# Leaving the first softmax map unscaled: a change to a hybrid SSD and differential-attention layer on one core

## The chip, the cores and the metric

The kernel runs on one core of a Trainium2 chip. A core has a matrix engine (TensorE, "PE" in the profile, its weight loads "PEld"), three engines for elementwise work (VectorE "DVE", ScalarE "ACT", GpSimd "POOL") and SyncE ("SP"), which here issues the DMA transfers. The metric is the device time of one execution in microseconds (us); lower is better.

## The reference, cut to what matters

The layer normalises its input, projects it, feeds an SSD (state space) half and an attention half, and multiplies the two halves, side by side, with an output matrix; a residual and a last LayerNorm follow. The change is in the attention half. Of it:

```python
def diff_attention(q, k, v, lam, slopes):
    ...
        probs = jax.nn.softmax(scores, axis=-1)
        w = probs[:, :, 0] - lam * probs[:, :, 1]
        return jnp.einsum("bhqs,bshe->bqhe", w.astype(v.dtype), v)
...
def rms_norm(x, g):
    xf = x.astype(jnp.float32)
    ms = jnp.mean(jnp.square(xf), axis=-1, keepdims=True)
    return (xf * lax.rsqrt(ms + RMS_EPS) * g).astype(x.dtype)
...
    o = diff_attention(q, k, v, lam, slopes)
    o = rms_norm(o, subln_g) * (1.0 - lam_init)
    y_attn = o.reshape(b, s, D_ATTN) * jax.nn.silu(g)
    mix = jnp.einsum("bse,ed->bsd", jnp.concatenate([y_ssm, y_attn], axis=-1), w_out.astype(h.dtype))
    return layer_norm(ALPHA * h + mix, ln_g, ln_b)
```

There are 8 attention heads, 1024 tokens, and 128 value channels for each head. Since the norm divides a head's output by its own root mean square, a factor that is the same for all channels of a token falls out of it, but for the epsilon that is added under the root.

## The kernel before

The program is written as lanes of work (generators), and a helper, the Loom, weaves them into one order of TensorE's instructions. Each lane emits instructions and yields the tiles that it needs next; the Loom keeps books of when each tile would be ready by its own cost estimates, and lets go on the first lane, by a table of ranks (`LANES`), whose next piece would not make TensorE wait. TensorE's order is pinned to that result; the other engines' order is set by the tile scheduler. All instructions go through one wrapper, so nearly all rows of the profile carry its line, L140, and are told apart by their tiles.

From 432 us on the program is attention, then the output projection. For each head and each block of 128 queries (`tb`, 8 per head, 64 in all) the lanes are:

- `scores` (L977): 8 matmuls into the two PSUM tiles `sc`; on VectorE a custom operation for each map (`p<-sc,dist`: ALiBi distance and row extremum `nm`); on ScalarE an Exp for each map (`p<-p,nm`), which leaves the row sums in `ls`.
- `combine` (L1012): `rs` is the reciprocal of the two sums, its second column times minus lambda; the first map `p0` is scaled by its reciprocal (on GpSimd; on ScalarE in head 7); then one VectorE instruction adds the second map (`p0 = p1*rs1 + p0`).
- `values` (L1028): 8 transposes of `p0` through a PSUM bank `bk`, a rounded copy `wh` on ScalarE and the rest `wl` on VectorE; after two blocks 24 matmuls (8 times `vh` with `wh`, `vh` with `wl`, `vl` with `wh`) give the head's output `o` for 256 queries.
- `finish` (L1066): after four blocks the RMS norm: the square `osq`, split into `osh` and `osl`, two matmuls with a matrix of ones (`ones_r`), the mean plus epsilon in `msq`, Ln and Exp for the root, one Newton step, gate and store (`yd<-o`).

Between these the Loom places what other work there is: until the end of head 6 the input projection of later heads (`bk<-hh,whi` and the like, weights loaded as `wst` and split by GpSimd into `wlo`), and after that the output projection `project_out` (L1241) in units of 128 tokens times half of the rows (`bk<-oh,oyh`; `ws` are its weight rows, split into `oh`/`ol` and `or`; `ys` its inputs, split into `oyh`/`oyl`). A unit of the first five token blocks sums in two PSUM banks, which are then added into the residual tile `xr` on VectorE, and this frees the banks. `xr` is the input, normalised on ScalarE, times `g_e`, plus `b_e` (two rows broadcast by DMA, then scaled once on ScalarE), both on GpSimd. The tiles `g_e`, `b_e` stand where tiles of the attention stood before, so their loads wait for those to be read.

```python
A.activation(p0, p0, AF.Copy, scale=rs[:, 0:1])                       # head 7
P.tensor_scalar(p0, p0, rs[:, 0:1], 1.0, op0=ALU.mult, op1=ALU.mult)  # other heads
yield p0
V.scalar_tensor_tensor(p0, p1, rs[:, 1:2], p0, op0=ALU.mult, op1=ALU.add)
```

Of the kernel before, what the change touches and what calls it, by code (L numbers as in the profile page):

```python
# [9 lines left out]
F32 = mybir.dt.float32  # L10
# [4 lines left out]
ALU = mybir.AluOpType  # L15
# [12 lines left out]
# rank of each lane, and how much later than estimated it takes its inputs to be ready  # L28
# [18 lines left out]
class Loom:  # L47
    """Weaves lanes of work into one instruction order.

    A lane is a generator that emits instructions and yields in between: nothing (it can go on),  # L50
    a tile (it can go on once the tile's last write is done), a function (once it holds) or a
    time (it lets other lanes go first for so long).
    When each tile is ready is estimated from the instructions emitted so far; the lane that
    goes on is the first one, by rank, that would not make TensorE wait."""
# [30 lines left out]
    def slot(self, key, start, cost):  # L85
        """The first gap of an engine that takes an instruction ready at start."""
        busy = self.busy.setdefault(key, [])
        i = len(busy)
        while i and busy[i - 1][1] > start:
            i -= 1  # L90
        while i < len(busy) and busy[i][0] - start < cost:
            start = max(start, busy[i][1])
            i += 1
        busy.insert(i, (start, start + cost))
        del busy[:-300]
        return start
# [33 lines left out]
class Engine:  # L130
    """An engine whose instructions are noted in the loom."""
# [21 lines left out]
class Pool:  # L153
    """A tile pool whose slots' reuse is noted in the loom; under are the pools whose place it takes."""
# [62 lines left out]
def hybrid_layer_kernel(  # L217
# [48 lines left out]
    # -|query - key| for every offset of a block of 128 queries  # L266
    dist = const.tile([128, 1920], F16, name="dist")

# [27 lines left out]
    class Block:  # L296
        """128 projected channels; evac(half, psum) takes each half of the sequence."""
# [8 lines left out]
    def weights():  # L306
        """Loads and splits the weights of a block while the one before it is computed."""
# [60 lines left out]
    # ================= embedding LayerNorm and bidirectional SSD =================  # L368
# [30 lines left out]
    def conv_block(b, when, dst_of, after):  # L399
        """Block b of x/B/C: raw projection, then convolution and SiLU into dst_of()."""  # L400
# [31 lines left out]
    def to_tokens(src, put):  # L432
        """Transposes src [128 ch, S]; put(half, psum [128 tokens, 4, 128])."""
# [48 lines left out]
    with tc.tile_pool(name="dp", bufs=1) as dp_, tc.tile_pool(name="p0", bufs=1) as p0_:  # L482
# [93 lines left out]
        def steps_lane():  # L576
            """Step sizes, decays and their sums within chunks."""
# [117 lines left out]
    def ssd(g):  # L695
# [72 lines left out]
        def maps():  # L768
            """Within-chunk maps of one head, four chunks at a time."""
# [96 lines left out]
    # ================= differential attention =================  # L866
# [8 lines left out]
    class Head:  # L875
        def __init__(self, h):
            self.pool = lambda: ep if h % 2 == 0 else att["op"]
            self.q, self.k, self.v, self.g = [], 0, 0, 0
            self.scored = self.summed = self.done = 0
# [3 lines left out]
    def free_since(h, what, n):  # L883
        """The tiles that head h overwrites are read no more."""
# [92 lines left out]
    def scores():  # L977
        """Unnormalised maps of 128 queries at a time."""
        for h, H in enumerate(heads_):
            m_h = 2.0 ** -(h + 1)  # L980
            for tb in range(8):
# [3 lines left out]
                ls = ap.tile([128, 2], F32, name="ls", bufs=2)  # L985
# [13 lines left out]
                for m in range(2):  # L999
# [6 lines left out]
                                 accum_out=ls[:, m:m + 1])  # L1006
# [5 lines left out]
    def combine():  # L1012
        """Difference of the two normalised maps, left in the first."""
        for _ in range(64):
# [3 lines left out]
            rs = ap.tile([128, 2], F32, name="rs", bufs=2)  # L1018
            V.reciprocal(rs, ls)
            V.tensor_mul(rs[:, 1:2], rs[:, 1:2], neg_lam)  # L1020
            if H is heads_[7]:
                A.activation(p0, p0, AF.Copy, scale=rs[:, 0:1])
            else:
                P.tensor_scalar(p0, p0, rs[:, 0:1], 1.0, op0=ALU.mult, op1=ALU.mult)
            yield p0
            V.scalar_tensor_tensor(p0, p1, rs[:, 1:2], p0, op0=ALU.mult, op1=ALU.add)
            maps_.append((H, tb, p0))

    def values():
        """Maps transposed and split; weighted sums of the values, 256 queries at a time."""  # L1030
        for _ in range(64):
# [31 lines left out]
            if n:  # L1063
                loom.add(finish(H, H.o, tb // 4))

    def finish(H, o, half):  # L1066
        """RMS norm over the head's 128 channels, gate, store."""
# [13 lines left out]
        V.tensor_scalar(ms, pms, 1.0 / 128, EPS, op0=ALU.mult, op1=ALU.add)  # L1081
# [4 lines left out]
        V.tensor_mul(ms, ms, rt)  # L1086
        V.tensor_scalar(ms, ms, -0.5, 1.5, op0=ALU.mult, op1=ALU.add)
        yield lambda: H.g == 1
        P.tensor_mul(o, o, H.gate[:, 512 * half:512 * half + 512])
        V.tensor_mul(rt, rt, ms)  # L1090
# [12 lines left out]
    # ================= output projection and LayerNorm =================  # L1103
# [3 lines left out]
    def late_rows():  # L1107
        """Places for the rows of the attention half: tiles of the last head, as they fall free."""
# [15 lines left out]
    def early_rows():  # L1124
        """The rows for the SSD half take the place of the normalised input."""
# [7 lines left out]
    def rows_out():  # L1133
        """Splits the rows of the output projection, half a row at a time."""
# [28 lines left out]
    def y_out():  # L1163
        """Splits the gated outputs of one unit, two units ahead of the products."""
# [20 lines left out]
    def residuals():  # L1185
        """ALPHA times the normalised input, token blocks in the order of their use."""
# [127 lines left out]
```

## Time and profile before

| | |
|---|---|
| time, 3 runs | 1234.62, 1236.5 and 1240.69 us; median 1236.5 |
| profiled execution | span 1236.1 us, which stands for its own time; 0.4 us below the median |
| busy, PE | 1176.0 us, 95% of the span |
| busy, DVE | 933.8 us, 76% |
| busy, ACT | 677.8 us, 55% |
| busy, POOL | 479.9 us, 39% |
| mean granted TensorE clock | 0.990 of full speed |
| chain that ended last | PE 11%, DVE 1%, all else under 1% of the span |

A busy share is the time in which an engine runs instructions; a wait is the idle time of an engine before an instruction, with the instruction that ended it. The clock is the share of full speed that TensorE was granted; where it reads near 0.5, matmuls take twice as long and still count as busy. The trace names an operation by its output and inputs, `p<-p,rs` for instance, with buffer numbers left out.

### The profile page before, as it was taken

Reading aid. Unit: us, or ns where it says so; the run is one execution under the profiler, and the core shown is the slowest. Engines: PE = TensorE matmul, PEld = TensorE weight load, DVE = VectorE, ACT = ScalarE, POOL = GpSimd, SP = SyncE. Lnnn points to the kernel's source line nnn. Section 1 sums busy time; section 2 is a strip of 40 time slices with the busy share of each in tenths; the row PEclk is TensorE's granted clock in tenths of the full one; section 3 lists DMA queues with packets and bytes.
Section 4 is the critical chain, followed back from the end, with each engine's and each line's share of the span. In section 5 each row is a group of like instructions: output and inputs, shape, how many; then the busy total and the mean of one; then the engine's idle time right before and its main releaser. Section 6 shows DMA issues by size and latency. Waiting matters only on the chain. (4 is left out here: it accounts for less than half of the span.)

```text
span 1236.1 us, 16398 instructions
## 1 busy us (share of the span) xinstructions
PE 1176.0 (95%) x5881; PEld 922.4 (75%) x5881; DVE 933.8 (76%) x1334; ACT 677.8 (55%) x1181; POOL 479.9 (39%) x404
## 2 busy tenths in 40 slices
PE   5998999899899999999999999999999998999997
PEld 3787666788567777777787777877777776778885
DVE  6687888867988568788788787887878889962334
ACT  4556356734457456665755656556656687641221
POOL 7422664323654323223332333233332429541354
PEclk9999999999899999999999999999999998999999
DMA  6113335522245421012112111121111263233221
GB/s 198 32 33 112 89 112 167 178 69 65 89 118 151 132 72 49 26 44 51 26 35 52 43 44 35 34 52 35 43 28 47 81 209 107 55 123 112 78 85 60
DMA packets 107591, 98.03 MB, mean 79 GB/s; under 512 B 9364, under 2 KB 79349, under 8 KB 107509
## 3 DMA queue, kind: packets, MB, share of 16 engines
q1 hardware_dynamic: 107509, 96.98, 27.2%
q8 instruction: 46, 0.75, 0.2%
q14 instruction: 36, 0.29, 0.1%
HBM read 75.85 MB, written 16.91 MB: 75 GB/s over the span
## 5 line engine op out<-in xcount | busy, mean ns | idle before, releaser
L140 PE MATMUL bk<-hh,whi 128*128 128x512 f32 x832 | 353.2, 425 | 0.6
L140 PE MATMUL bk<-hl,whi 128*128 128x512 f32 x832 | 327.0, 393 | 3.2 <-POOL hl L140 2.8
L140 PE MATMUL bk<-hh,wlo 128*128 128x512 f32 x832 | 328.0, 394 | 0.0
L140 ACT ACTIVATE p<-p,nm 128x1024 f32<-128x1024 f32 x128 | 146.8, 1148 | 121.7 <-DVE nm L140 121.0
L140 POOL TENSOR_TENSOR wlo<-wst,whi 128x512 fp32r<-128x512 f32 x104 | 161.5, 1557 | 126.9 <-ACT whi L140 109.2
L140 POOL TENSOR_SCALAR p<-p,rs 128x1024 f32<-128x1024 f32 x56 | 64.5, 1152 | 350.4 <-DVE rs L140 287.5
L140 PEld LDWEIGHTS bk<-hh,wlo 128*128 128x128 f32 x832 | 156.6, 188 | 34.9
L140 PEld LDWEIGHTS bk<-hl,whi 128*128 128x128 f32 x832 | 157.7, 190 | 32.9 <-POOL hl L140 5.4
L140 PEld LDWEIGHTS bk<-hh,whi 128*128 128x128 f32 x832 | 157.7, 190 | 32.7 <-issue 5.8
L140 DVE CUSTOM_DVE_ANT_0 p<-sc,dist 128x1024 f32<-128x1024 f32 x128 | 151.3, 1218 | 11.6 <-PE sc L140 10.9
L140 DVE SCALAR_TENSOR_TENSOR p<-p,rs,p 128x1024 f32<-128x1024 f32 x64 | 128.4, 2007 | 22.1 <-POOL p L140 18.0
L140 DVE TENSOR_TENSOR wl<-bk,wh 128x512 fp32r<-128x512 f32 x128 | 87.0, 684 | 15.6 <-ACT wh L140 13.7
L140 ACT CAST wh<-bk 128x512 fp32r<-128x512 f32 x128 | 74.1, 580 | 43.2 <-PE bk L140 42.7
L140 ACT CAST whi<-wst 128x512 fp32r<-128x512 f32 x104 | 64.2, 620 | 46.9 <-PE bk L140 38.1
L140 PE MATMUL bk<-ident,p 128*128 128x128 f32 x512 | 79.4, 278 | 4.7 <-DVE wl L140 2.7
L140 PEld LDWEIGHTS bk<-ident,p 128*128 128x128 f32 x512 | 61.6, 142 | 29.5 <-DVE wl L140 6.2
L140 PE MATMUL bk<-wh,vh 128*128 128x256 f32 x256 | 74.6, 291 | 0.0
L140 PE MATMUL bk<-wl,vh 128*128 128x256 f32 x256 | 72.2, 282 | 0.7 <-DVE wl L140 0.7
L140 PE MATMUL sc<-kk,q 128*128 128x512 f32 x256 | 72.3, 393 | 0.0
L140 PE MATMUL bk<-wh,vl 128*128 128x256 f32 x256 | 72.0, 281 | 0.0
L140 ACT ACT_TABLE_LOAD x42 | 53.9, 1283 | 25.5 <-DVE t L140 15.7
L140 PEld LDWEIGHTS bk<-xt,t 128*128 128x128 f32 x256 | 45.8, 192 | 26.5 <-issue 15.0
(217 smaller groups left out, 2188.1 us busy)
## 6 DMA issues: line engine op xcount, KB each, us to landing
wst<-in_w_in_dram SPq DMA_DIRECT2D x104, 256.0 KB, 3.0
t<-acs_d SPq DMA_DIRECT2D x64, 256.0 KB, 3.5
ws<-in_w_out_dram SPq DMA_DIRECT2D x32, 256.0 KB, 3.1
ys<-yd SPq DMA_DIRECT2D x32, 256.0 KB, 3.0
xb<-in_x_dram SPq DMA_DIRECT2D x8, 512.0 KB, 6.2
zd<-zs SPq DMA_DIRECT2D x16, 256.0 KB, 2.5
gz<-zd SPq DMA_DIRECT2D x16, 256.0 KB, 3.3
yd<-ys SPq DMA_DIRECT2D x16, 256.0 KB, 2.8
```

Of the source, the lines that this page charges most:

```text
L140: r = f(*args, **kw)
```

## The change

The first map stays as the exponentials are. With sums l0 and l1 the head's output is then l0 times what it was, if the second map is added with the factor -lambda * l0 / l1. The norm takes the factor l0 out again, when epsilon is multiplied by l0 squared. Since in `finish` channels lie on partitions and queries along the row, and in `scores` queries lie on partitions, the 512 values eps * l0^2 of four blocks go to DRAM (`ed`, one word each, turned) and come back as a row that is broadcast to all partitions (`er`).

In `scores` one tile `ls` of 4 x 2 sums now serves four blocks. In `combine` the scaling of `p0` and the yield behind it are gone; in `finish` `er` is added in place of the constant, and the Newton step is written in three instructions for four. The compiler object gets a smaller scratch for dynamic DMA. (Comments and docstrings also go; they are left out here.)

```diff
     def scores():
...
-                ls = ap.tile([128, 2], F32, name="ls", bufs=2)
+                if tb % 4 == 0:
+                    ls = ap.tile([128, 4, 2], F32, name="ls", bufs=2)
...
-                                 accum_out=ls[:, m:m + 1])
+                                 accum_out=ls[:, tb % 4, m:m + 1])
...
     def combine():
...
-            rs = ap.tile([128, 2], F32, name="rs", bufs=2)
-            V.reciprocal(rs, ls)
-            V.tensor_mul(rs[:, 1:2], rs[:, 1:2], neg_lam)
-            if H is heads_[7]:
-                A.activation(p0, p0, AF.Copy, scale=rs[:, 0:1])
-            else:
-                P.tensor_scalar(p0, p0, rs[:, 0:1], 1.0, op0=ALU.mult, op1=ALU.mult)
-            yield p0
-            V.scalar_tensor_tensor(p0, p1, rs[:, 1:2], p0, op0=ALU.mult, op1=ALU.add)
+            rs = ap.tile([128, 1], F32, name="rs", bufs=2)
+            V.reciprocal(rs, ls[:, tb % 4, 1:2])
+            V.scalar_tensor_tensor(rs, rs, ls[:, tb % 4, 0:1], neg_lam, op0=ALU.mult, op1=ALU.mult)
+            V.scalar_tensor_tensor(p0, p1, rs, p0, op0=ALU.mult, op1=ALU.add)
             maps_.append((H, tb, p0))
+            if tb % 4 == 3:
...
+                e2 = ap.tile([128, 4], F32, name="e2", bufs=2)
+                V.scalar_tensor_tensor(e2, ls[:, :, 0], EPS, ls[:, :, 0], op0=ALU.mult, op1=ALU.mult)
+                ed = dr.tile([4, 128], F32, name="ed", bufs=2)
+                with nc.allow_non_contiguous_dma(reason="512 words"):
+                    dma(ed.rearrange("t p -> p t"), e2)
+                er = ap.tile([128, 512], F32, name="er", bufs=2)
+                dma(er, ed.rearrange("t p -> (t p)").partition_broadcast(128))
+                H.er.append(er)
...
-                loom.add(finish(H, H.o, tb // 4))
...
+                loom.add(finish(H, H.o, H.er[tb // 4], tb // 4))
...
-        V.tensor_scalar(ms, pms, 1.0 / 128, EPS, op0=ALU.mult, op1=ALU.add)
+        V.scalar_tensor_tensor(ms, pms, 1.0 / 128, er, op0=ALU.mult, op1=ALU.add)
...
         V.tensor_mul(ms, ms, rt)
-        V.tensor_mul(ms, ms, rt)
-        V.tensor_scalar(ms, ms, -0.5, 1.5, op0=ALU.mult, op1=ALU.add)
+        V.scalar_tensor_tensor(ms, ms, -0.5, rt, op0=ALU.mult, op1=ALU.mult)
+        V.scalar_tensor_tensor(rt, ms, 1.5, rt, op0=ALU.add, op1=ALU.mult)
...
-        V.tensor_mul(rt, rt, ms)
...
-    nc = _bacc.Bacc("TRN2", target_bir_lowering=False, num_devices=1)
+    nc = _bacc.Bacc("TRN2", target_bir_lowering=False, num_devices=1,
+                     dynamic_dma_scratch_size=1024)
```

The Loom's books change with it, and so does the order. Two places follow, and one on SyncE.

**VectorE, the same block of the steady part (the 28th, the last of a half head).** Before, the custom operations of one block (`ISA` rows), then the reciprocal of the two sums and the addition of the maps, with a `wl` between them:

```order
L140 ISA p1_6204,nm_6189<-sc_6194,dist_80 128x1024
L140 ISA nm_6189 128x1
L140 RECIPROCAL rs_6260<-ls_6190 128x2
L140 TENSOR_TENSOR rs_6260<-rs_6260,neg_lam_83 128x1
L140 TENSOR_TENSOR wl_6239<-bk_6240,wh_6238 128x4x128
L140 SCALAR_TENSOR_TENSOR p0_6201<-p1_6204,rs_6260,p0_6201 128x1024
```

After, with the epsilon values `e2` ahead:

```order
L140 ISA p1_6271,nm_6257<-sc_6261,dist_80 128x1024
L140 ISA nm_6257 128x1
L140 SCALAR_TENSOR_TENSOR e2_6346<-ls_5985 128x4
L140 RECIPROCAL rs_6342<-ls_5985 128x1
L140 SCALAR_TENSOR_TENSOR rs_6342<-rs_6342,ls_5985,neg_lam_83 128x1
L140 SCALAR_TENSOR_TENSOR p0_6268<-p1_6271,rs_6342,p0_6268 128x1024
```

The reciprocal is of one column, the product takes l0 in as well, and nothing of another engine stands between `rs` and the addition.

**TensorE, end of head 6.** Before, the last of the 24 matmuls of head 6's values (`bk_8978`), then the last 24 projection matmuls (`bk_8984<-hh1_0...` to `hh1_7...`) with 8 transposes among them, then the ones matmuls (`osh`, `osl`), the scores, 4 transposes, and the first matmuls of an output unit (`bk_9246`, `bk_9247`):

```order
L140 MATMUL bk_8978<-wh_8886,vl_8046 128x256
L140 MATMUL bk_8984<-hh1_0_108,whi_8722 128x512
L140 MATMUL bk_8984<-hl1_0_124,whi_8722 128x512
...
L140 MATMUL bk_8984<-hl1_7_131,whi_8726 128x512
L140 MATMUL bk_8984<-hh1_7_115,wlo_8727 128x512
L140 MATMUL bk_9040<-osh_9036,ones_r_76 128x512
L140 MATMUL bk_9040<-osl_9037,ones_r_76 128x512
L140 MATMUL sc_9098<-kk_8598,q_8406 128x512 x2
L140 MATMUL sc_9101<-kk_8598,q_8406 128x512 x2
...
L140 MATMUL sc_9101<-kl_8599,q_8406 128x512
L140 MATMUL bk_9114<-ident_69,p0_8992 128x128 x4
L140 MATMUL bk_9246<-oh0_9126,oyh_9224 128x512
L140 MATMUL bk_9247<-oh1_9132,oyh_9224 128x512
```

After, the last of head 6's values is `bk_9160`; the output unit in these rows is the second one (`bk_9334`, `bk_9335`; the first, `bk_9028` and `bk_9029`, stands ahead of the values now):

```order
L140 MATMUL bk_9160<-wh_9055,vl_7892 128x256
L140 MATMUL bk_9217<-ident_69,p0_9123 128x128 x4
L140 MATMUL bk_9240<-ident_69,p0_9123 128x128 x4
L140 MATMUL bk_9214<-osh_9210,ones_r_76 128x512
L140 MATMUL bk_9214<-osl_9211,ones_r_76 128x512
L140 MATMUL sc_9255<-kk_8467,q_8267 128x512 x2
L140 MATMUL sc_9258<-kk_8467,q_8267 128x512 x2
...
L140 MATMUL sc_9258<-kl_8468,q_8267 128x512
L140 MATMUL bk_9271<-ident_69,p0_9173 128x128 x4
L140 MATMUL bk_9278<-ident_69,p0_9173 128x128 x4
L140 MATMUL bk_9334<-oh0_8908,oyh_9018 128x512
L140 MATMUL bk_9335<-oh1_8914,oyh_9018 128x512
```

The projections have been used up before this place, the first output unit has moved ahead of it, and the ones matmuls stand behind 8 transposes alone.

**SyncE, the same stretch, after.** Its issues in order; `ed_9069` and `er_9071` are head 6's last epsilon row, and the `ws` rows behind them are output weights (`ws_8978` and `ws_8984` of rows 14 and 15, which the first output unit's last matmuls use):

```order
L140 DMA ys_9218<-yd2_134 128x512
L140 DMA ys_9224<-yd2_134 128x512
L140 DMA ed_9069<-e2_9067 128x4x1
L140 DMA er_9071<-ed_9069 128x512
L140 DMA ws_8978<-in_w_out_dram 128x512
L140 DMA ws_8984<-in_w_out_dram 128x512
L140 DMA ws_8990<-in_w_out_dram 128x512
L140 DMA ys_9463<-yd3_135 128x512
L140 DMA ws_8996<-in_w_out_dram 128x512
L140 DMA ws_9002<-in_w_out_dram 128x512
L140 DMA ys_9469<-yd3_135 128x512
L140 DMA g_e_9302<-in_ln_emb_g_dram 128x1024
```

`ed` waits for `e2`, and `er` for `ed`'s landing; before, no such pair stood among the issues.

## Rows read from the trace of the kernel before

**Rows 1.** Busy time by stretch: core start:end, length, then us busy of each engine.
```profile
432.40:980.00 547.60, 545.59 (x2921) 430.28 (x2919) 439.14 (x658) 333.74 (x580) 166.96 (x123) 1.00 0.17 43
980.00:1000.00 20.00, 17.61 (x104) 13.97 (x104) 17.78 (x25) 13.63 (x24) 5.34 (x5) 1.00 0.43 133
1000.00:1031.50 31.50, 27.46 (x146) 21.91 (x146) 27.06 (x41) 28.91 (x47) 15.86 (x11) 0.99 0.71 234
1031.50:1038.00 6.50, 6.50 (x18) 5.25 (x19) 6.46 (x7) 4.89 (x8) 6.50 (x5) 0.54 0.25 82
...
1080.00:1087.45 7.45, 4.93 (x27) 3.77 (x25) 4.99 (x8) 4.99 (x8) 3.71 (x3) 1.00 0.65 208
1087.45:1092.50 5.05, 5.05 (x19) 4.17 (x20) 4.01 (x7) 2.31 (x4) 1.73 (x2) 0.66 0.40 124
1092.50:1228.30 135.80, 135.77 (x598) 110.41 (x596) 48.82 (x84) 30.44 (x48) 56.55 (x45) 1.00 0.28 87
```

**Rows 2.** The chain that ended last, in order of time: start us, us, what.
```profile
1080.08 3.89 DMA xr<-in_x_dram
...
1087.45 29.35 PE bk L140 x136
```

**Rows 3.** What TensorE waited for, 980 to 1092 us: total, times, longest.
```profile
PE bk L140 <- DVE wl L140: 3.4, 3, 2.5
```

**Rows 4.** What VectorE waited for, 432 to 980 us.
```profile
DVE p L140 <- POOL p L140: 17.0, 20, 1.1
```

**Rows 5.** Groups of the page on the maps: count | busy, mean ns | idle before.
```profile
L140 ACT ACTIVATE p<-p,nm 128x1024 f32<-128x1024 f32 x128 | 146.8, 1148 | 121.7 <-DVE nm L140 121.0
...
L140 POOL TENSOR_SCALAR p<-p,rs 128x1024 f32<-128x1024 f32 x56 | 64.5, 1152 | 350.4 <-DVE rs L140 287.5
...
L140 DVE CUSTOM_DVE_ANT_0 p<-sc,dist 128x1024 f32<-128x1024 f32 x128 | 151.3, 1218 | 11.6 <-PE sc L140 10.9
L140 DVE SCALAR_TENSOR_TENSOR p<-p,rs,p 128x1024 f32<-128x1024 f32 x64 | 128.4, 2007 | 22.1 <-POOL p L140 18.0
```

**Rows 6.** The tile p, 432 to 980 us: duration ns min/median/max.
```profile
L140 DVE SCALAR_TENSOR_TENSOR p<-p,rs,p x54: 1268/2304/2350, 443.4 to 966.0; 128x1024 f32<-128x1024 f32 x54
```

**Rows 7.** Timeline at the end of head 6: start us, us, engine, operation.
```profile
1001.47 0.28 PE L140 MATMUL bk<-wh,vl 128*128 128x256 f32 x1
...
1001.78 0.33 SPq L140 DMA_DIRECT2D g_e<-in_ln_emb_g_dram  x1
...
1003.68 0.60 PE L140 MATMUL bk<-ident,p 128*128 128x128 f32 x4
...
1008.05 0.39 PE L140 MATMUL bk<-osh,ones_r 128*128 128x512 f32 x1
...
1008.28 0.39 PE L140 MATMUL bk<-osl,ones_r 128*128 128x512 f32 x1
```

**Rows 8.** Timeline at the start of the second output unit.
```profile
1021.91 0.81 ACT L140 ACTIVATE xr<-xr,nmr,rstd 128x512 f32<-128x512 f32 x1
...
1022.79 1.28 POOL L140 TENSOR_TENSOR xr<-xr,g_e 128x512 f32<-128x512 f32 x1 [1.14 <-ACT xr L140]
...
1030.77 1.27 DVE L140 TENSOR_TENSOR xr<-xr,bk 128x512 f32<-128x512 f32 x2
...
1031.50 0.80 PE L140 MATMUL bk<-oh,oyh 128*128 128x512 f32 x1 [3.33 <-DVE xr L140]
```

**Rows 9.** The tile msq, whole run: duration ns min/median/max.
```profile
L140 ACT ACTIVATE rt<-msq x16: 617/632/635, 490.8 to 1108.2; 128x512 f32<-128x512 f32 x16
L140 DVE TENSOR_SCALAR msq<-msq x16: 417/425/428, 495.8 to 1112.6; 128x512 f32<-128x512 f32 x16
```

**Rows 10.** DMA issues: count, KB each, median us from issue to landing.
```profile
g_e<-in_ln_emb_g_dram SPq DMA_DIRECT2D x1, 512.0 KB, 3.9
...
acs_d<-acs_row SPq DMA_DIRECT2D x16, 8.0 KB, 1.5
...
bro<-in_A_log_fwd_dram SPq DMA_DIRECT2D x1, 8.0 KB, 7.2
```

More of the change, by code (lines that the diff above doesn't have):

```diff
@@ L878, in __init__ @@
             self.q, self.k, self.v, self.g = [], 0, 0, 0
+            self.er = []
             self.scored = self.summed = self.done = 0
@@ L1063, in values, with finish @@
             if n:
-                loom.add(finish(H, H.o, tb // 4))
-    def finish(H, o, half):
+                loom.add(finish(H, H.o, H.er[tb // 4], tb // 4))
+    def finish(H, o, er, half):
         h = heads_.index(H)
```

## The prediction

> **What bounds the kernel now.** I read the page first: TensorE is busy 95% of the span, so an edit on the other engines can give back only what TensorE stands idle, or runs at its lower clock, because of them. The busy time by stretch says where that is. Attention runs from about 432 to 1092 us. In the first 547.60 us of it TensorE is busy for 545.59 [rows 1]: only 2.0 us are idle there, although GpSimd's scaling of the first map takes 64.5 us over the run and VectorE waits 17.0 us for it [rows 4, 5]. That is the first thing to see: the step that the change removes is a wait of VectorE, and hardly one of TensorE.
>
> The loss is at the end of head 6 and of head 7. TensorE is idle 20.00 - 17.61 = 2.4 us in 980 to 1000, 31.50 - 27.46 = 4.0 in 1000 to 1031.5, and 7.45 - 4.93 = 2.5 in 1080 to 1087.45 [rows 1]. Behind the last two of these stretches its granted clock falls to the lower level (1.2 instead of 2.4 GHz): it was 0.54 for 6.50 us and 0.66 for 5.05 us [rows 1], which costs 0.46 x 6.50 = 3.0 and 0.34 x 5.05 = 1.7 us; the 0.99 ahead of them is another 0.3. After 1087.45 the chain of waits is TensorE work back to back [rows 2], and the stretch to 1228.3 holds no idle time [rows 1]. So everything that VectorE, ScalarE and GpSimd cost TensorE from 432 us on is 2.0 + 8.9 + 5.0 = about 16 us, and a gain above that is not to be had. The profiled execution is its own time here: 1236.1 us, 0.4 under the median of the runs, and the sum is made against it.
>
> **The change, step by step.**
>
> Scaling gone. A block's chain on the other engines was two custom operations of 1.22 us, two Exp of 1.15, the reciprocal, the scaling at 1.15 and the addition at 2.0 in the mean [rows 5]. The scaling and its hand-overs leave, some 1.3 us a block. TensorE waits for that chain only where other work has run out, so the steady part can give 0 to 2.0 us [rows 1]; since a part of the 2.0 us is waits for values and not for maps, I take -1.5. In 980 to 1000 one of three waits is for the maps; I take -0.7 of 2.4.
>
> Beside it, the addition itself: 1268 ns at best, 2304 in the median [rows 6], so something shares its way to memory; the scaling has always ended before the addition starts and can't be that something. What the addition overlaps with (GpSimd's splitting of weights) stays. The Trainium skill, GPSIMD Engine Reference, section 1 (Specifications), says that GpSimd shares its SBUF interfaces with VectorE, with contention for VectorE instructions that have two SBUF inputs. The two durations agree with it; by the rule 64.5 us less of GpSimd would speed other VectorE instructions, by the row TensorE can't show more than the 2.0 us.
>
> Norm. `finish` loses one of its VectorE steps, the 0.425 us one [rows 9], for 16 halves; `e2` adds a very small one. Both lie in slack: nothing, bounds -0.4 to +0.2 us in each of the two end stretches, where TensorE waits for VectorE.
>
> Epsilon row. 16 times, SyncE issues `ed` once `e2` is there, waits for its landing, then issues `er`. The trace has no store of single words. From below, a small store to DRAM landed in 1.5 us; from above, a small broadcast load of parameters landed in 7.2; a broadcast of a row to all partitions took 3.9 [rows 10]. I take 1.5 + 3.9 = 5.4 us for the pair, and 14.4 as the upper end. It is needed at `msq`, behind 24 value matmuls and the ones matmuls; the second alone came 6.5 us after the last value matmul (1001.75 to 1008.28 [rows 7]). So it is hidden, at nothing, and SyncE's queue stands 1.5 us longer in each half head.
>
> The smaller scratch: no queue of the profile uses it; nothing.
>
> Order at the end of head 6. This is the big term. The excerpts of TensorE's order show that before, 24 projection matmuls, scores, transposes and most of an output unit lay between the last value matmul of head 6 and the second output unit. That second unit needs the banks of the first, which come free when VectorE adds them into `xr`; and `xr` needs `g_e`, whose load is issued at the end of head 6's values (1001.78, against their end at 1.47 + 0.28 = 1001.75 [rows 7]). Before, the addition came at 1030.77 and the second unit waited 3.33 us for it [rows 8], although 29 us had gone by since the values' end. After, the first unit stands ahead of the values, and what is left between is 16 transposes, the 2 ones matmuls and 8 score matmuls. Ten matmuls at the spacing 1008.28 - 1008.05 = 0.23, and four groups of transposes at under 0.60 [rows 7], are about 4 us of work.
>
> How long will the wait be? On ScalarE `xr` stands behind the Ln of `msq`, so behind the ones matmuls. These came 6.5 us after the last value matmul before, with 24 projection matmuls beside; the copies, squares and splits that they wait for stay, and stand behind more `wl` work on VectorE's queue after, so 6.2 to 9.0, I take 7.5. Then `msq` and Ln (0.63 each, about [rows 9]), `xr` on ScalarE 0.81, two GpSimd steps of 1.28, VectorE's addition 0.64 [rows 8]: 5.3 us, and 1.2 for six hand-overs and an instruction of VectorE in the way: 14.0 us. The second bank needs a `wl` behind that addition, 1.5 to 2 us more, against 0.23 of work. Idle: 14.0 + 2.0 - 4.0 = 12.0, with the bounds 11 to 13. The clock has fallen after each long wait of TensorE here; I put 3.0 as for the 3.33 us wait, bounds 1.7 to 5. The stretch is then 12.0 + 3.0 = 15.0 against 4.0 + 3.3 = 7.3 us before: +7.7.
>
> End of head 7. Before, TensorE waited 2.5 us for a `wl` [rows 3], because ScalarE had `xr` ahead of it, whose load took 3.89 us [rows 2]. After, the last blocks' transposes stand further apart, but that `xr` load is behind an `ed` on SyncE. I allow 0 to 4 us for wait and clock together, 2 in the middle, against 2.5 + 1.7 = 4.2: -2.2.
>
> Sum: -1.5 - 0.7 + 7.7 - 2.2 = +3.3, 1236.1 + 3.3 = 1239.4 us, say 1239.5.
>
> **The rivals.**
>
> Faster. ScalarE and VectorE have less to do at the end of head 6, and the norm's leg is not what ends last: then `g_e` is. It lands 3.9 us after the last value matmul [rows 10]; two scalings of about 1.15, `xr` 0.81, GpSimd 2.56, VectorE 0.64 give 10.2 us, less 4 of work: 6.2 idle and 3.0 for the clock, +1.9 against before. With the waits at head 7 gone (-4.2), those in 980 to 1000 too (-2.4), and the steady part at -2.0, that is -6.7, 1229.4; without the clock's fall 1226.4. For it: VectorE was busy 27.06 of the 31.50 us [rows 1], so relief there counts. Against it: the removed work is GpSimd's, which was busy for half of that stretch.
>
> Slower, SyncE held. `ed` and `er` stand ahead of the weight rows 14 and 15, which the first output unit's last matmuls use, some 5 to 9 us behind `e2` in TensorE's order. `ed` 1.5, a row's load of up to 3.9 [rows 10], the cast and the split give about 7.4: from `ed` at 3 us on it decides. If `ed` takes 7.2, TensorE stands 13.1 - 7 = about 6 us, with part of a clock's fall 7: 1246.5. For it: 512 words of 4 bytes are many small writes, and no row excludes it. The Trainium skill, DMA: Bandwidth & Descriptors, section Specifications, says that transfers under 512 bytes are done by read-modify-write, which speaks for the slow end. The trace has no store of that kind to weigh it with; 8 KB stores at 1.5 us are the nearest.
>
> Slower, `er` late. If both take 7.2 us, 14.4 exceeds the 9 or so between `e2` and `msq`; VectorE then stands up to 5 us in 16 halves, and TensorE for 1 to 2 of them: 1256 to 1271.
>
> **How the numbers follow.** A change of this kernel's time under about 0.5% (1230.3 to 1242.7) can't be told from none. Forecast 0.57 (1234 to 1245; 0.46 of it within 0.5%, 0.11 above), faster 0.20 (0.17 below 1230.3), SyncE held 0.17 (0.15 above 1242.7), `er` late 0.06. That makes faster 0.17, same 0.51, slower 0.32. The range takes in the faster rival's 1229.4 and the held one with its bounds, 1229 to 1249; under it and over it about 0.1 each.
>
> **What would show it.** Right: idle time of TensorE in one piece of 10 us or more a little after the last value matmuls of head 6, ended by VectorE's `xr`, with the clock at its lower level behind it; no wait of VectorE for a DMA at `msq`; the steady part with under 2 us idle; VectorE's waits for GpSimd's `p` gone. Wrong: the second output unit starts within 8 us of the last value matmul (faster); `ws` named as what TensorE or ScalarE waits for behind `ed` (held); landings of `ed` above 3 us. The forecast falls altogether if the order printed here isn't what runs, or if the steady part's idle time grows, which no row suggests.

## The result, and the profile after

The changed kernel takes 1252.9 us in the median of 4 runs (1252.31 to 1255.41), the kernel before 1236.67 (4 runs, 1234.62 to 1240.69): the ratio is 1.0125, 95% interval 1.0102 to 1.0148. The change is slower by some 16 us, and the time lies above the stated range, 1229 to 1249.

The scaling is gone as meant. GpSimd is busy for 415.0 us instead of 479.9, VectorE for 890.9 instead of 933.8. The addition of the maps, which took 2007 ns in the mean and 128.4 us in all [rows 5], now takes 1324 ns in the mean and 84.7 us in all, and in the steady part, by the tile p (duration min/median/max, as in [rows 6]):

```profile
L140 DVE SCALAR_TENSOR_TENSOR p<-p,rs,p x54: 1283/1285/1289, 442.7 to 972.5; 128x1024 f32<-128x1024 f32 x54
```

Busy time by stretch, after (columns as in [rows 1]):

```profile
432.40:980.00 547.60, 544.28 (x2935) 434.30 (x2934) 402.70 (x649) 334.74 (x579) 110.05 (x71) 1.00 0.21 51
980.00:1007.69 27.69, 24.94 (x133) 19.72 (x133) 20.31 (x33) 18.79 (x31) 4.51 (x3) 1.00 0.41 119
1007.69:1014.34 6.65, 0.40 (x2) 0.00 (x0) 2.38 (x4) 1.74 (x4) 1.26 (x1) 0.79 0.63 198
1014.34:1022.67 8.33, 8.33 (x41) 6.75 (x42) 6.85 (x12) 5.27 (x9) 0.00 (x0) 0.76 0.24 73
1022.67:1035.30 12.63, 5.32 (x27) 2.95 (x25) 9.24 (x17) 11.83 (x22) 6.24 (x5) 0.87 0.77 242
1034.03:1040.00 5.97, 5.50 (x14) 4.03 (x15) 5.97 (x8) 3.59 (x5) 5.16 (x4) 0.60 0.58 212
1035.30:1108.18 72.88, 68.91 (x348) 54.55 (x349) 54.10 (x81) 34.71 (x60) 37.45 (x26) 0.98 0.22 63
1108.18:1114.70 6.52, 0.40 (x2) 0.00 (x1) 0.69 (x1) 2.06 (x4) 1.17 (x1) 0.68 0.61 120
1114.70:1122.00 7.30, 7.30 (x21) 5.52 (x22) 4.78 (x6) 1.85 (x4) 2.62 (x3) 0.58 0.57 183
1122.00:1243.90 121.90, 121.90 (x539) 99.06 (x537) 44.72 (x78) 29.30 (x46) 55.91 (x45) 1.00 0.29 88
```

The steady part lost a little instead of giving something: 547.60 - 544.28 = 3.3 us idle against 2.0. The reader is to see two short stretches. In 1007.69 to 1014.34 and in 1108.18 to 1114.70 TensorE is busy for 0.40 us: two holes of 6.3 and 6.1 us, one ahead of the last values of head 6, one at the end of head 7, where it waited 2.5 us before. Behind the first the granted clock is 0.76 in the mean for 8.33 us (2.0 us lost), behind the second 0.58 for 7.30 us (3.1 us lost): part of each stretch ran at the lower level, 1.2 GHz. Together 12.4 + 5.1 = 17.5 us, against 2.5 + 1.7 = 4.2 before. What the forecast put its money on, the stretch between the last value matmul (1022.22 + 0.29 = 1022.51) and the start of the second output unit, is 1022.67 to 1035.30: 12.63 - 5.32 = 7.3 us idle, and the clock behind its longest wait, 0.60 for 5.97 us, costs 2.4 more.

These sums are rough. Added up over all stretches from 432 us on, with the 4.0 us idle between 1035 and 1108 us, what TensorE loses is about 21 us more than before, and the span grew by 15.7. The ends of matmuls are modelled in the trace; whether that is the difference, no run shows.

TensorE in that stretch, after, its last value matmul and the instructions that it waited for (idle time before, and what ended it, in brackets):

```profile
1022.22 0.29 PE L140 MATMUL bk<-wh,vl 128*128 128x256 f32 x1
...
1025.82 0.47 PE L140 MATMUL bk<-osh,ones_r 128*128 128x512 f32 x1 [1.55 <-DVE wl L140]
1026.92 0.50 PE L140 MATMUL bk<-osl,ones_r 128*128 128x512 f32 x1 [0.64 <-DVE osl L140]
...
1034.03 0.79 PE L140 MATMUL bk<-oh,oyh 128*128 128x512 f32 x1 [3.99 <-DVE xr L140]
1035.30 0.79 PE L140 MATMUL bk<-oh,oyh 128*128 128x512 f32 x1 [0.47 <-DVE wl L140]
```

What TensorE waited for most from 432 us on, after (total, times, longest, as in [rows 3]):

```profile
PE bk L140 <- DVE wl L140: 8.5, 4, 6.1
PE bk L140 <- DVE xr L140: 7.2, 3, 4.0
PE sc L140 <- DVE nm L140: 7.1, 2, 6.3
```

Who made it wait is read one engine further back each time. The timeline of after in front of the first hole's end (the trace cuts the number off names, so `e2` reads `e`):

```profile
996.52 0.37 SPq L140 DMA_DIRECT2D ed<-e  x1
...
1004.39 0.32 SPq L140 DMA_DIRECT2D er<-ed  x1
...
1004.81 3.75 SPq L140 DMA_DIRECT2D ws<-in_w_out_dram  x3
...
1010.64 1.29 ACT L140 CAST oh<-ws 128x512 fp32r<-128x512 f32 x2 [9.10 <-DMA ws<-in_w_out_dram]
...
1011.96 1.19 DVE L140 TENSOR_TENSOR ol<-ws,oh 128x512 fp32r<-128x512 f32 x1 [8.66 <-ACT oh L140]
...
1013.07 1.21 DVE L140 CUSTOM_DVE_ANT_0 p<-sc,dist 128x1024 f32<-128x1024 f32 x1
```

SyncE issued `ed` at 996.52 and stood until 1004.39, when it could issue `er`; only then came the weight rows `ws`. ScalarE stood 9.10 us for them (`oh`), VectorE 8.66 us for ScalarE, and the custom operation that frees the score banks stood behind that on VectorE's queue: hence TensorE's wait for `nm`. At the end of head 7 the chain of waits of after names the load itself:

```profile
1101.23 11.30 DMA xr<-in_x_dram
```

An `xr` load whose issue came 1.8 us after that of an `ed` took 11.30 us, where it had been 3.89 before [rows 2]. DMA issues of after (columns as in [rows 10]), and SyncE's waits for `ed`:

```profile
ws<-in_w_out_dram SPq DMA_DIRECT2D x32, 256.0 KB, 3.0
...
er<-ed SPq DMA_DIRECT2D x16, 256.0 KB, 5.6
...
ed<-e SPq DMA_DIRECT2D x16, 2.0 KB, 8.1
```

```profile
SPq L140 <- DMA ed<-e: 133.0, 16, 10.5
```

`ed`, 2 KB, lands 8.1 us after its issue in the median, and SyncE stood 133.0 us for the 16 of them, 8.3 us each.

### The profile page after: what moved, and what is told of

Read it like the earlier page. It is cut to its first block, busy times and chain, and to the rows that moved or that the text cites. A ratio compares the mean times of both kernels' runs of the same rounds, so it can differ in the third digit from the quotient of the medians.

```text
span 1251.8 us, 16298 instructions
## 1 busy us (share of the span) xinstructions
PE 1175.1 (94%) x5881; PEld 924.0 (74%) x5881; DVE 890.9 (71%) x1334; ACT 671.9 (54%) x1173; POOL 415.0 (33%) x348
## 4 chain that ended last, share of the span: by engine, by line
PE 55%; DVE 6%; DMA 4%; ACT 3%; issue 1%; POOL 1%; SPq 0%; DVEq 0%; POOLq 0%; ACTq 0%
PE bk L140 44%; PE sc L140 11%; DVE p L140 1%; ACT p L140 1%; DMA xr<-in_x_dram 1%; DMA ys<-yd 1%; DMA ws<-in_w_out_dram 1%; DVE t L140 1%; DMA ed<-e 1%; DMA t<-acs_d 1%; DVE wl L140 1%; DVE osl L140 0%; DVE yt L140 0%; POOL ol L140 0%; DMA b_e<-in_ln_emb_b_dram 0%
## 5 line engine op out<-in xcount | busy, mean ns | idle before, releaser
L140 POOL TENSOR_TENSOR wlo<-wst,whi 128x512 fp32r<-128x512 f32 x104 | 151.9, 1465 | 380.1 <-ACT whi L140 330.7
L140 PE MATMUL bk<-ident,p 128*128 128x128 f32 x512 | 79.0, 277 | 12.5 <-DVE wl L140 6.1
L140 DVE SCALAR_TENSOR_TENSOR p<-p,rs,p 128x1024 f32<-128x1024 f32 x64 | 84.7, 1324 | 2.2
L140 POOL TENSOR_TENSOR o<-o,gate 128x512 f32<-128x512 f32 x16 | 31.1, 1946 | 165.5 <-ACT osq L140 165.5
L140 ACT ACT_TABLE_LOAD x42 | 53.9, 1283 | 25.8 <-DVE t L140 15.8
```

The source lines that it names most:

```text
L140: r = f(*args, **kw)
```

## The experiments

Four theories were set against each other. HOLD: the cost is `ed`. It splits into STAND (SyncE waits for `ed`'s landing and holds what is queued behind) and WRITES (512 one-word writes slow the transfers issued behind them, whoever waits). ORDER: TensorE's new order at the end of head 6, the forecast's big term. Where nothing else is said, TensorE's order of instructions is that of the changed kernel, row for row; the order of SyncE's issues can differ, and is told where it matters. Ratios are to the runs of the kernel before that were made beside each.

**The pair taken out (e_const).**

```diff
+    erc = ap.tile([128, 512], F32, name="er")
+    P.memset(erc, EPS)
...
-                e2 = ap.tile([128, 4], F32, name="e2", bufs=2)
...
-                    dma(ed.rearrange("t p -> p t"), e2)
...
-                dma(er, ed.rearrange("t p -> (t p)").partition_broadcast(128))
-                H.er.append(er)
+                H.er.append(erc)
```

> The changed kernel without ed and er: the epsilon row is a constant tile, so the factor l0 squared on epsilon is left out. TensorE's order is that of the changed kernel, instruction for instruction. Theory HOLD (SyncE stands 8 to 10 us for each landing of ed and the loads behind it come late): the 6.25 us wait of TensorE for nm at the end of head 6 with the low clock behind it, and most of the 6.1 us wait at the end of head 7 with its low clock, are gone; 1252.9 falls by 14 to 21 us, to 1232 to 1239. Theory ORDER (the new order of TensorE leaves too little work at the end of head 6): the time stays at 1246 to 1253.

1237.38 us (10 runs, 1235.88 to 1245.51), ratio to before 1.0003, 0.9983 to 1.0024. The loss is gone, to within the interval, with the new order in place: ORDER by itself falls, HOLD stands.

**The load issued later (e_late).** The line that issues `er` was moved to where a head's values are done.

> The changed kernel with the load er issued later, where the head's values are done, so that other loads stand between ed and er on SyncE's queue; all else and TensorE's order as in the changed kernel. HOLD, by SyncE's standing alone: nearly all of the loss goes as in the run without ed and er, to 1232 to 1241. HOLD, by the small writes of ed themselves, which slow the loads issued behind it (an xr load behind ed took 11.3 us): it stays above 1244. ORDER: 1246 to 1253.

1253.59 us, ratio 1.0114 (1.0087 to 1.0141). It tells nothing apart: the scheduler put `er` back, and SyncE's order came out as in the changed kernel. It is a second sample of that kernel.

**The pair alone, in the order of before (b_ed).**

```diff
             maps_.append((H, tb, p0))
+            if tb % 4 == 3:
...
+                nc.sync.dma_start(ed.rearrange("t p -> p t"), e2)
+                nc.sync.dma_start(er, ed.rearrange("t p -> (t p)").partition_broadcast(128))
```

> The kernel before, with a pair of transfers like ed and er added for each half head, behind the addition of the maps of its fourth block; er is read by nobody; the smaller scratch as in the changed kernel. TensorE's order is that of before. HOLD: the pair alone costs time also here, where urgent loads stand behind it at the ends of heads 6 and 7: 1240 to 1250. ORDER: 1236 to 1238.5, since nobody reads er and the order is the old one.

1241.16 us (10 runs, 1236.27 to 1246.86), ratio 1.0019 (0.9998 to 1.0040). The median lies in the range of HOLD, but the interval takes in no change: inconclusive. `ed` landed in 9.0 us there too. So the same slow store costs 16 us in one order and at most 5 in the other. That what is issued behind it decides is the reading of this, not a test of it.

**The scaling alone taken out (b_noscale).** The books of the Loom are kept as before, so TensorE's order is that of before; epsilon isn't multiplied by l0 squared. (`GV`, `GA` and `GP` enter an instruction in the books and emit none.)

```diff
-            V.reciprocal(rs, ls)
-            V.tensor_mul(rs[:, 1:2], rs[:, 1:2], neg_lam)
+            GV.reciprocal(rs, ls)
+            GV.tensor_mul(rs[:, 1:2], rs[:, 1:2], neg_lam)
             if H is heads_[7]:
-                A.activation(p0, p0, AF.Copy, scale=rs[:, 0:1])
+                GA.activation(p0, p0, AF.Copy, scale=rs[:, 0:1])
             else:
-                P.tensor_scalar(p0, p0, rs[:, 0:1], 1.0, op0=ALU.mult, op1=ALU.mult)
+                GP.tensor_scalar(p0, p0, rs[:, 0:1], 1.0, op0=ALU.mult, op1=ALU.mult)
+            nc.vector.reciprocal(rs[:, 1:2], ls[:, 1:2])
+            nc.vector.scalar_tensor_tensor(rs[:, 1:2], rs[:, 1:2], ls[:, 0:1], neg_lam, op0=ALU.mult, op1=ALU.mult)
```

> The kernel before with the first map left unscaled and the ratio of sums on the second; epsilon is left as it is, not times l0 squared. The Loom's books are kept as before, so TensorE's order is that of before. The forecast's own terms for the scaling (-1.5 in the steady part, -0.7 in 980 to 1000) and perhaps a part of the 2.5 us wait at the end of head 7: 1230 to 1236. A rival, that the scaling hid nothing and its going moves other work into worse places: 1237 to 1241.

1237.64 us (10 runs, 1236.96 to 1243.39), ratio 0.9996 (0.9979 to 1.0014): no gain, in the range of the rival. The steady part, and TensorE's wait for `wl` in it:

```profile
432.40:980.00 547.60, 542.05 (x2927) 433.12 (x2925) 405.35 (x659) 339.24 (x583) 103.61 (x70) 1.00 0.17 44
```

```profile
PE bk L140 <- DVE wl L140: 4.6, 7, 0.7
```

The steady part is idle for 547.60 - 542.05 = 5.6 us, more than the 2.0 of before: the split of the transposes comes 0.6 to 0.7 us late for the ones matmuls, once in each of seven halves. I put this down to another order in VectorE's and ScalarE's queues; that was not tested. (The profiled execution took 1242.09 us and is one of the slower ones of the ten, but a wait that comes back in every half is not chance.)

**The store without anyone waiting for it (ed_only), and the load without the store (er_only).**

In ed_only:

```diff
-                dma(er, ed.rearrange("t p -> (t p)").partition_broadcast(128))
-                H.er.append(er)
+                H.er.append(erc)
```

In er_only, where `edc` is written once at the start:

```diff
-                    dma(ed.rearrange("t p -> p t"), e2)
...
-                dma(er, ed.rearrange("t p -> (t p)").partition_broadcast(128))
+                dma(er, edc.rearrange("t p -> (t p)").partition_broadcast(128))
```

> The changed kernel with the stores ed as they are, but without the loads er: the epsilon row is a constant tile, so the factor l0 squared on epsilon is left out. SyncE no longer stands for ed's landing; the 512 one-word writes are still made. TensorE's order is that of the changed kernel. Theory STAND (the cost is that SyncE waits for ed and holds what is queued behind it): 1236 to 1240, as without the pair. Theory WRITES (the one-word writes slow the loads that are issued behind them on the queue, as xr behind ed took 11.3 us): 1244 to 1253, with the wait at the end of head 7 still there.

> The changed kernel with the 16 loads er as they are, from a row in DRAM that is written once at the start with the constant epsilon; no ed, so the factor l0 squared is left out and no load waits for a store. STAND and WRITES both: 1236 to 1240. A rival, that the broadcast load er itself (256 KB, 5.6 us to landing) takes the queue from the weight rows: 1242 or more.

ed_only: 1249.93 us (5 runs, 1246.28 to 1253.98), ratio 1.0099 (1.0065 to 1.0132). er_only: 1235.42 us (10 runs, 1232.44 to 1238.50), ratio 0.9979 (0.9963 to 0.9995), 0.6 us under the range expected. So, by the medians of e_const and er_only, 12.5 to 14.5 us come with the writes although nobody waits for them. STAND has what is left, some 3 us by the medians; the intervals of ed_only and of the changed kernel overlap, so it may be nothing or a few us more. The timeline of ed_only shows how, at both places:

```profile
995.87 0.37 SPq L140 DMA_DIRECT2D ed<-e  x1
...
999.71 1.48 SPq L140 DMA_DIRECT2D ws<-in_w_out_dram  x3
...
1007.58 1.30 ACT L140 CAST oh<-ws 128x512 fp32r<-128x512 f32 x2 [6.67 <-DMA ws<-in_w_out_dram]
```

```profile
1095.42 1.51 SPq L140 DMA_DIRECT2D ed<-e  x1
...
1097.04 0.45 SPq L140 DMA_DIRECT2D xr<-in_x_dram  x1
...
1107.43 0.81 ACT L140 ACTIVATE xr<-xr,nmr,rstd 128x512 f32<-128x512 f32 x1 [6.79 <-DMA xr<-in_x_dram]
```

SyncE is free now and issues `ws` 3.8 us after `ed`; still ScalarE gets the row only at 1007.58, 7.9 us after the issue (a `ws` takes 3.0 in the median of after). From the issue of `ed` to that cast it is 11.7 us, against 14.1 in the changed kernel: SyncE's standing is worth 2.4 us here. The `xr` load issued at 1097.04 is there at 1107.43. In er_only the holes are gone (TensorE's longest wait from 432 us on is 2.4 us), and the stretch behind 1100 has 0.45 us idle:

```profile
1100.00:1228.00 128.00, 127.55 (x564) 103.38 (x562) 48.77 (x85) 31.70 (x51) 58.04 (x47) 1.00 0.30 94
```

**The store on another queue (e_actq).**

```diff
-                    dma(ed.rearrange("t p -> p t"), e2)
+                    nc.scalar.dma_start(ed.rearrange("t p -> p t"), e2)
...
```

> The changed kernel in full, but ed is issued on ScalarE's queue; er stays on SyncE, which still stands until ed has landed. TensorE's order is that of the changed kernel. WRITES, on the queue alone (loads wait behind the words only on the same queue): the xr load at the end of head 7 lands in about 4 us again and what is left is SyncE's standing at the end of head 6, 1240 to 1248. WRITES, on the transfer engines whatever the queue: 1249 to 1254, as in the changed kernel.

1247.27 us (7 runs, 1241.60 to 1250.49), ratio 1.0080 (1.0057 to 1.0104). The time lies in the range of the theory of one queue, but the trace does not bear it out. The profiled run is the fastest of the seven, and SyncE issued `ws` ahead of `er` in it, so that `ws` did not stand behind the wait for `ed`:

```profile
993.98 0.37 ACTq L1031 DMA_DIRECT2D ed<-e  x1
...
997.82 1.48 SPq L140 DMA_DIRECT2D ws<-in_w_out_dram  x3
...
1005.06 1.29 ACT L140 CAST oh<-ws 128x512 fp32r<-128x512 f32 x2 [6.07 <-DMA ws<-in_w_out_dram]
```

The weight rows, on SyncE's queue and 3.8 us behind an `ed` on ScalarE's, came some 7 us after their issue all the same. In the chain of waits of the same kernel, at the end of head 7:

```profile
1095.37 7.50 DMA ws<-in_w_out_dram
```

There the `xr` load happened to be issued ahead of `ed`, and the weights behind it took the delay. So the writes hold up loads of another queue too. The queue of ScalarE, which carries nothing but `ed`, also tells the number of pieces: 8448 packets, 528 for each of the 16 stores.

**The same 2 KB in larger pieces (e_row, e_row2, e_dvt).** In the first two TensorE turns the four columns into the free half of the bank of the values, and `ed` is stored as 4 rows of 512 bytes; e_row does it ahead of the 24 value matmuls, e_row2 behind them. In e_dvt VectorE turns them in blocks, and `ed` is 16 pieces of 128 bytes.

For e_row and e_row2:

```diff
+                loom.tc.keep_in_program_order(nc.tensor.transpose(po[0:4, 256:384], e2, ident))
...
+                nc.scalar.copy(es, po[0:4, 256:384])
...
+                nc.sync.dma_start(ed, es)
```

For e_dvt, where `e2` is 128 x 32 with four columns in use:

```diff
+                nc.vector.transpose(et, e2)
...
+                for b in range(4):
+                    nc.sync.dma_start(ed[:, 32 * b:32 * b + 32], et[32 * b:32 * b + 4, :])
```

> The changed kernel in full, but the 4 epsilon columns are turned by one more TensorE transpose for each half head (16 of 0.11 us, 1.7 us in all), so ed is a store of 4 rows of 512 bytes in place of 512 words; er as before, now issued at the start of the values. The rest of TensorE's order is that of the changed kernel. If the size of ed's writes is the cause, by STAND or WRITES: ed lands in 1.5 to 2.5 us and the time is 1237 to 1242. If any way through DRAM costs this much: 1247 or more. A rival: er now comes too late for msq and VectorE waits for it, 1242 to 1250.

> As the run with 512-byte rows (e_row), but the transpose of the epsilon columns stands behind the 24 value matmuls, where TensorE waits for nothing that reads the bank. e_row's wait for es (9.2 us up to 1000, and the low clock behind its longest) goes; ed lands in 2 to 2.5 us, er in 4, about when the ones matmuls are done. WRITES: 1236 to 1241. If the row comes too late for msq at the end of head 6: up to 1244. If it isn't the writes: 1249 or more.

> The changed kernel in full, but VectorE turns the epsilon columns in 32 x 32 blocks (one more instruction of some 0.2 us for each half head) and ed is stored as 16 pieces of 128 bytes by four issues in place of 512 words by one; er as before. TensorE's order is that of the changed kernel. WRITES: the pieces land in 2 to 4 us, and the time is 1236 to 1242. If the small store's round trip and not the number of its pieces is the cause: 1249 or more.

e_row: 1253.72 us, ratio 1.0132 (1.0100 to 1.0164). That lies where any way through DRAM was to cost this much, but the trace names another cause, from 432 to 1000 us:

```profile
PE bk L140 <- ACT es L1062: 9.2, 13, 4.6
```

TensorE waited for `es`, the copy out of the bank that the values then fill; with the low clock behind its longest wait (4.6 us) and 16 transposes this is most of the loss, made by the edit itself, and the two holes of the changed kernel are not in its trace. e_row2 takes that wait away: 1238.47 us (10 runs, 1235.05 to 1242.70), ratio 1.0008 (0.9986 to 1.0029). e_dvt: 1239.52 us (10 runs, 1236.27 to 1242.05), ratio 1.0008 (0.9988 to 1.0027). Both compute all that the changed kernel computes, with a store and a waiting load in the same half heads, and the loss is gone. In e_row2 the store also stands elsewhere, behind the values and so behind `ws` and `xr` at the two holes; its time alone does not tell size from place. e_dvt keeps the place at the end of head 6. SyncE's issues there, ScalarE's cast, and two of TensorE's waits from 432 us on:

```profile
995.29 1.27 SPq L1036 DMA_DIRECT2D ed<-et  x4
...
998.89 1.48 SPq L140 DMA_DIRECT2D ws<-in_w_out_dram  x3
...
1000.54 0.33 SPq L140 DMA_DIRECT2D er<-ed  x1
```

```profile
1001.79 1.27 ACT L140 CAST oh<-ws 128x512 fp32r<-128x512 f32 x2 [1.06 <-DMA ws<-in_w_out_dram]
```

```profile
PE bk L140 <- DVE xr L140: 4.3, 2, 2.6
PE bk L140 <- DVE wl L140: 3.4, 4, 1.6
```

`ws` is issued 3.6 us behind `ed`, as in ed_only (3.8), and ScalarE has the row 2.9 us after the issue, where it was 7.9 there: the same loads behind the same 2 KB, in other pieces (and by four issues for one).

**No transfer at all (e_mm, e_mm2).** GpSimd spreads the columns on a diagonal, and one more matmul with the matrix of ones adds them into the norm's bank; `er` is then the diagonal, 128 x 512. e_mm lets the Loom make its own order; e_mm2 keeps that of the changed kernel. The matmuls of e_mm:

```diff
-        T.matmul(pms, ones_r, lo, start=False, stop=True)
+        T.matmul(pms, ones_r, lo, start=False, stop=False)
+        T.matmul(pms, ones_r, er.rearrange("p t n -> p (t n)"), start=False, stop=True)
```

> The change without any transfer: GpSimd spreads the four epsilon columns on a diagonal (128 x 4 x 128), and one more matmul with the matrix of ones for each half head adds them into the norm's bank. 16 matmuls of 0.23 us are 3.7 us more work for TensorE; the Loom makes another order. HOLD by ed: the loss is gone, 1236.5 + 3.7 less what the new order gives or takes, 1233 to 1245. If the loss of the changed kernel came from elsewhere: above 1247.

> The diagonal matmul of e_mm (no transfer at all), but put into the changed kernel's order of TensorE by hand, with the Loom's books kept as they are there: 16 matmuls of 0.23 us more. Against er_only's 1235.4 that is 3.7 us: 1237 to 1242. e_mm's 1252 came with an order of its own; if instead the diagonal itself (GpSimd's 16 products and the matmul) costs it: 1249 or more.

e_mm: 1252.34 us, ratio 1.0115 (1.0083 to 1.0147), where the loss was to lie if it came from elsewhere than `ed`. e_mm2: 1243.27 us (10 runs, 1239.90 to 1245.61), ratio 1.0048 (1.0031 to 1.0064). The 9 us between them come with the Loom's other order, so an order can cost that much, though that of the changed kernel does not (e_const); which of its places costs them was not followed up. e_mm2 is 1.3 us above the expected range; in its trace TensorE waits once 3.4 us for `rt`, which was not foreseen.

No full version beat the kernel before: er_only is 0.2% under it, but leaves the factor out, and e_row2 and e_dvt are level with it.

## Why the prediction was wrong, step by step

**The step that failed** is the price of the store `ed`: "I take 1.5 + 3.9 = 5.4 us for the pair, and 14.4 as the upper end", and from it that "SyncE's queue stands 1.5 us longer in each half head", which went into the sum as nothing. The store landed in 8.1 us and the row in 5.6, 13.7 together, almost the upper end, and SyncE stood 8.3 us each time. That the row itself is hidden held (see below); what the sum left out is what the loads behind the store pay, the two holes and the clock behind them: 17.5 us in the trace, and 15.5 by the medians (1252.9 against 1237.38 in e_const). I had taken the nearest row by destination and size (an 8 KB store), not by the number of pieces: 512 words. With 4 rows of 512 bytes for the same 2 KB SyncE issues `er` 1.2 us after `ed`, less than the 1.5 that I had assumed. SyncE's issues in the steady part of e_row2:

```profile
653.21 0.27 SPq L1068 DMA_DIRECT2D ed<-es  x1
654.39 0.34 SPq L1070 DMA_DIRECT2D er<-ed  x1
```

The forecast named this case as a rival, SyncE held, with the point from which it decides (`ed` at 3 us) and a price of about 7 us, at 0.17. The place and the victims were right: the weight rows 14 and 15, ScalarE's cast behind them. Two parts of it were too small. It counted the end of head 6 alone, and the same store stands ahead of the `xr` load at the end of head 7, where I had written that the load "is behind an `ed` on SyncE" and allowed 0 to 4 us; it was 6.1 and 3.1 for the clock. And its mechanism was SyncE's standing; ed_only shows that most of the loss stays when SyncE doesn't stand. Of the signs that the forecast named, those of this rival came: `ed` landed above 3 us, and ScalarE waited for `ws` behind it. The Trainium skill, DMA: Bandwidth & Descriptors, section Specifications, says that transfers under 512 bytes are done by read-modify-write. The rule spoke against this change. The runs agree with its direction (512 pieces of 4 bytes 8.1 us, 4 pieces of 512 bytes 1.2); whether that is the mechanism, and not the number of pieces as such, no run here shows, and e_dvt's 128-byte pieces, under the limit too, cost nothing that can be measured.

**The rest of the sum.** With a quickly landing store the same change takes 1238.5 and 1239.5 us (e_row2, e_dvt), where the forecast said 1239.5. Its terms, read from the changed kernel, were less good than their sum, so the agreement is luck in part:

- Steady part, -1.5: wrong in sign. It is +1.3 in the changed kernel (3.3 us idle against 2.0), and b_noscale shows 5.6. That growth was itself a sign against the forecast.
- 980 to 1000, -0.7: not given. Ahead of the first hole, 980 to 1007.69, 27.69 - 24.94 = 2.8 us are idle, against 2.4 before.
- End of head 6, 12 us of idle time behind the last value matmul: 7.3, in the pieces 0.67, 1.55, 0.64, 3.99 and 0.47, and 2.4 for the clock where 3.0 was set. That is 9.7 and not 15.0, against 7.3 before. The ones matmuls came 4.4 us after that matmul and not 7.5, so the norm's leg was shorter, and the second unit started at 11.5 us and not at 14.0. VectorE's `xr` ended the longest piece, as forecast.
- End of head 7 without the slow store: no hole in er_only, where 0.45 us are idle and the clock is full behind 1100 us. The allowance of 2 us was too much; nearly the full 4.2 us of before are given back.
- Between 1035 and 1108 us of the changed kernel TensorE is idle for 4.0 us, mostly for `xr`; the forecast had nothing there.
- `er` late: it did not happen. VectorE's waits for `msq` in the whole run of after name the norm's bank and ScalarE's `rt`, never a transfer:

```profile
DVE msq L140 <- ACT rt L140: 14.2, 14, 1.4
...
DVE msq L140 <- PE bk L140: 6.9, 7, 1.8
```

- The addition of the maps: I said that what it overlaps with, GpSimd's splitting of weights, stays, and that the scaling has no part in it. The splits stay, but the slow additions went: 1283 to 1289 ns in every block of the steady part. Timelines of VectorE and GpSimd, first before, then after, show why:

```profile
746.37 1.12 POOL L140 TENSOR_SCALAR p<-p,rs 128x1024 f32<-128x1024 f32 x1 [5.54 <-DVE rs L140]
...
747.46 1.28 POOL L140 TENSOR_TENSOR wlo<-wst,whi 128x512 fp32r<-128x512 f32 x1
747.53 2.30 DVE L140 SCALAR_TENSOR_TENSOR p<-p,rs,p 128x1024 f32<-128x1024 f32 x1
```

```profile
448.55 1.28 DVE L140 SCALAR_TENSOR_TENSOR p<-p,rs,p 128x1024 f32<-128x1024 f32 x1
448.65 2.33 POOL L140 TENSOR_TENSOR wlo<-wst,whi 128x512 fp32r<-128x512 f32 x1 [0.36 <-ACT whi L140]
```

Of the two, the one that begins later is the long one. In the steady part of before, 40 of the 54 additions begin 0.02 to 0.52 us behind a GpSimd instruction with two inputs that still runs (34 times a split `wlo`, 6 times `o<-o,gate`), and all 40 take 2.2 to 2.35 us; the other 14 begin beside none and take 1.27 to 1.29. In after none of the 54 begins behind one. In the block shown, the end of the scaling freed the addition and GpSimd's queue in the same moment; without the scaling the two no longer start together. Some 44 us of VectorE time were saved by it, and the time shows none of them.

Where did the gain of the removed work go? Nowhere that the time shows: it was off TensorE's path. VectorE's waits for GpSimd's `p` are gone, as forecast, but of the 16 us that other engines cost TensorE before, the scaling had little: b_noscale, which removes it in the order of before, is level with before, and its interval leaves at most 2.6 us.

**A smaller slip.** The sum was made against the span. In the runs of the changed kernel, listed with both, the time is 1.7 us above the span (1253.49 to 1251.8), so the profiled execution's own time was not its span.

## What to carry to other kernels

Price a DMA by its pieces and not by its bytes alone: look for a row with as many pieces of that size, and if there is none, take the dear end where a queue of loads stands behind it. Then look at what is issued behind it within its landing time, on every queue, at the places where TensorE has no other work; a slow store that nobody waits for can still be the cost. And work taken off an engine that the bound engine does not wait for gives nothing, while the new order that it brings can cost or give several us.

## What the runs showed of the hardware that was not expected

A store of 512 single words (2 KB) landed 8.1 us after its issue (10.1 in the median of ed_only); behind one of 4 rows of 512 bytes SyncE could issue the load that waits for it after 1.2. Loads of 256 KB that were issued up to 4 us behind the 512 words came 7 to 11 us after their issue in place of 3 to 4, and also when the store was on another engine's queue. Behind 16 pieces of 128 bytes, at the same place, it was 2.9.

VectorE's addition of two maps and a GpSimd instruction with two inputs did not run side by side at speed: the one that began second took up to 1.0 us longer (2.3 in place of 1.28), and a first addition kept its 1.28.
